# One shared wait for the score matmuls of a pair of MoBA heads

## The chip, the cores and the metric

The kernel runs on one core of a Trainium2 chip. The metric is the device time of one execution in microseconds (us), as the median of several runs. Engines are named as in the profile: PE is TensorE (PEld its weight loads), DVE is VectorE, ACT is ScalarE, POOL is GpSimd, SP is SyncE, whose queue issues the DMAs.

## The reference, cut to what matters

The reference is a two-layer decoder trunk on 256 tokens of width 1024. A layer normalises its input, modulates it by a conditioning vector, projects it by one wide matrix, runs two groups of attention heads, gates their outputs, projects back, normalises again and adds the result to its input.

The change concerns one of the two groups, the eight MoBA heads of width 64. The sequence is 256 and the MoBA block is 256, so every query has its own block alone, and for these heads the reference comes down to causal softmax attention with a linear position bias:

```python
s_own = jnp.einsum('hqd,hkd->hqk', q, k_own)
d_own = t[:, None] - pos[None, :]
s_own = jnp.where(d_own >= 0, s_own - slope_m[:, None, None] * d_own, NEG)
p = softmax(s_own)
o_m = jnp.einsum('hqb,hbd->hqd', p, v_own)
```

The other group, eight NSA heads, computes three such attentions a head (compressed, selected, window) and mixes them by gates.

## The kernel before, in words

All values are fp32. The large projections (helper `mm3`, L400 to L402) take three matmuls a product, from a high and a low part of each operand; weights come by DMA into `raw` (7 buffers) and are split by ACT (`hi`, L365) and DVE (`lo`, L373, or both parts on DVE, L367 and L373). While the first layer runs, the second layer's conditioning is computed too (the weights `w_ada`, by DVE at L234 and by PE at L217, L241 and L253).

Attention goes by blocks of two heads. There are four MoBA blocks a layer (`moba_block`) and four NSA blocks (`nsa_block`). The two heads of a MoBA block lie in partitions 0 to 63 and 64 to 127 of the same tile `qm` and `km`, so head 0 uses one half of PE's rows and head 1 the other. Queries come in two tiles of 128. A block issues four score matmuls (L636) in this order: head 0 with query tile 0 (128 keys), head 1 with query tile 0, head 0 with query tile 1 (256 keys), head 1 with query tile 1. The profile counts two records for each, so a block has eight. Head 0's scores go to one PSUM bank and head 1's to another; both have the tag `sc`, of which there are two banks, so a block takes both. Then `softmax` reads each head's bank in two spans by DVE (L546, with the bias and the row minimum), ACT does the exponentials (L549), and DVE or ACT scales (L560, L557). `transposed` puts the scaled scores through PE (L569) and copies them back (L575 on ACT, L573 on DVE), four matmuls multiply them by the values (L647), and `gate_out` multiplies by the gate (L656, L659, L660).

The banks `sc` are shared with the NSA blocks (L604, L605), with the compression (`ph` in `compress_out`, `sc` in `cmp_attn`) and with the last third of an output projection. A bank is free once its last reader is done. A matmul that writes a bank waits for that reader alone; so before the change head 0's matmuls wait for the reader of their bank, and head 1's for the reader of theirs.

Apart from the start of the first layer, whose order is written out by hand, the order on each engine is made by a planner when the kernel is built: in a model of the run it lets each engine take, of the instructions that are ready by then, the one that was traced first. `PLAN` gives the order of tracing, and steps lie far apart in it, so PE fills waits with matmuls of projections traced later. On the chip every engine goes through its own list in order. The helper `beside(mms, lasts)` makes each matmul of a list depend on the finished instructions `lasts`, and keeps the matmuls in their order among themselves; it does not forbid other matmuls between them. The other callers give it real `lasts` (`self.scaled`, `self.copies`); the score matmuls of MoBA give it an empty list.

Of the kernel before, what the change touches and what calls it, by code (L numbers as in the profile page):

```python
# [26 lines left out]
T_PAD = 16  # L27
# [41 lines left out]
class Trunk:  # L69
    def __init__(self, tc, ins, out):  # L70
        self.tc = tc
        self.nc = tc.nc
        self.I = ins
        self.out = out
        self.depth = ins["w_ada"].shape[0]
        self.n = 0
        self.how = ""
        self.used = set()
        self.copies, self.scaled = [], []
        self.parts, self.pv, self.z = {}, {}, [None, None]  # L80

    def pool(self, name, bufs=1, **kw):
# [371 lines left out]
    def compress_out(self, l):  # L454
        nc = self.nc
        sp = self.sp
        R = self.cmpR
        w1v = []
        for n in ("w_ck1", "w_cv1"):
            w1 = self.tl(self.rp, [P, 16, HD], "raw")  # L460
            nc.sync.dma_start(w1, self.I[n][l].rearrange("(m p) c -> p m c", p=P))
            w1v.append(w1)
        w2 = self.tl(self.mp, [P, P], "w2")
        nc.sync.dma_start(w2[0:HD, 0:HD], self.I["w_ck2"][l])
        nc.sync.dma_start(w2[0:HD, HD:P], self.I["w_ck2"][l])
        nc.sync.dma_start(w2[HD:P, 0:HD], self.I["w_cv2"][l])
        ph = self.tl(self.ps, [P, 512], "sc", bufs=2)
        for m in range(16):
            for i in range(2):
                nc.tensor.matmul(ph[i * HD:(i + 1) * HD, :33], w1v[i][:, m, :],  # L470
                                 R[:, i, m % 8, m // 8:m // 8 + 33],
                                 start=(m == 0), stop=(m == 15))
        hid = self.tl(sp, [P, 32], "hid", bufs=1)
        pb = self.tl(sp, [P, 1], "pbias", bufs=1)
        nc.vector.tensor_copy(pb, ph[:, 32:33])
        nc.vector.tensor_scalar_add(hid, ph[:, :32], pb)
        u = self.tl(sp, [P, 32], "gu", bufs=1)
        nc.vector.tensor_mul(u, hid, hid)
        nc.vector.tensor_scalar(u, u, 0.044715, 1.0, op0=OP.mult, op1=OP.add)
        nc.vector.tensor_mul(u, u, hid)  # L480
        nc.scalar.activation(u, u, AF.Tanh, scale=0.7978845608028654)
        nc.vector.tensor_scalar(u, u, 1.0, 0.5, op0=OP.add, op1=OP.mult)
        gel = self.tl(sp, [P, NG, 16], "gelu", bufs=1)
        nc.vector.tensor_mul(gel.rearrange("p g t -> p (g t)"), u, hid)
        grep = self.tl(sp, [P, NG, 4, 16], "gelr", bufs=1)
        for g in range(NG):
            nc.vector.tensor_copy(grep[HD:P, g], gel[HD:P, g:g + 1, :].broadcast_to([HD, 4, 16]))
        pk = self.tl(self.ps, [P, 512], "tr", bufs=2)
        nc.tensor.matmul(pk[:, :32], w2[0:HD, :], gel[0:HD].rearrange("p g t -> p (g t)"),
                         start=True, stop=True)  # L490
        nc.vector.tensor_copy(self.kbd[0:HD, :, 0:16],
                              pk[0:HD, :32].rearrange("p (g t) -> p g t", g=NG))
        nc.vector.tensor_copy(self.kbd[HD:P, :, 16:32],
                              pk[HD:P, :32].rearrange("p (g t) -> p g t", g=NG))
        pv = self.tl(self.ps, [P, 512], "tr", bufs=2)
        nc.tensor.matmul(pv[:, :HD], grep[HD:P].rearrange("p g j t -> p (g j t)"),
                         w2[HD:P, 0:HD], start=True, stop=True)
        self.vx = self.tl(self.mp, [P, NH, HD], "vx")
        nc.vector.tensor_tensor(
            self.vx, pv[:, :HD].unsqueeze(1).broadcast_to([P, NH, HD]),  # L500
            self.hmask.unsqueeze(2).broadcast_to([P, NH, HD]), op=OP.mult)

    def cmp_attn(self):
        nc = self.nc
        pt = self.tl(self.ps, [P, 512], "tr", bufs=2)
        for b in range(NBLK):
            nc.tensor.matmul(pt[b * 32:b * 32 + 32, :S], self.kbd[:, b // 2, :],
                             self.qn[:, b, :], start=True, stop=True)
        st = self.tl(self.wp, [P, 512], "S")
        nc.scalar.copy(st[:, :S], pt[:, :S])  # L510
        sc = self.tl(self.ps, [P, 512], "sc", bufs=2)
        for qt in range(NT):
            nc.tensor.transpose(sc[:, qt * P:(qt + 1) * P], st[:, qt * P:(qt + 1) * P], self.ident)
        n = NT * NH
        s = self.tl(self.wp, [P, n, T_PAD], "S")
        sv = s.rearrange("p n t -> p (n t)")
        nc.vector.tensor_add(sv, sc[:, :n * T_PAD], self.cbias.rearrange("p q h t -> p (q h t)"))
        mx = self.tl(self.sp, [P, n], "cmx", bufs=1)
        nc.vector.tensor_reduce(mx, s, axis=AX.X, op=OP.max)
        nc.vector.tensor_tensor(s, s, mx.unsqueeze(2).broadcast_to([P, n, T_PAD]), op=OP.subtract)  # L520
        nc.scalar.activation(sv, sv, AF.Exp)
        sm = self.tl(self.sp, [P, n], "csm", bufs=1)
        nc.vector.tensor_reduce(sm, s, axis=AX.X, op=OP.add)
        nc.vector.reciprocal(sm, sm)
        nc.vector.tensor_mul(sm, sm, self.valid.rearrange("p q h -> p (q h)"))
        nc.vector.tensor_mul(sm.rearrange("p (q h) -> p q h", q=NT),
                             sm.rearrange("p (q h) -> p q h", q=NT),
                             self.gate.rearrange("p q (h i) -> p q h i", i=3)[:, :, :, 0])
        nc.vector.tensor_mul(s, s, sm.unsqueeze(2).broadcast_to([P, n, T_PAD]))
        pt = self.tl(self.ps, [P, 512], "tr", bufs=2)  # L530
        for qt in range(NT):
            nc.tensor.transpose(pt[:, qt * P:(qt + 1) * P],
                                sv[:, qt * P:(qt + 1) * P], self.ident)
        self.pct = self.tl(self.mp, [P, S], "pct")
        nc.scalar.copy(self.pct, pt[:, :S])


    def softmax(self, sc, h, spans, w):

        nc = self.nc  # L540
        n = len(spans)
        s = self.tl(self.wp, [P, 512], "S")
        mn = self.tl(self.sp, [P, n], "mn")
        sm = self.tl(self.sp, [P, n], "sm")
        for i, (a, b) in enumerate(spans):
            nc.vector.tensor_tensor_reduce(  # L546
                out=s[:, a:b], in0=sc[:, a:b], in1=self.bias[:, h, S - (b - a):S],
                scale=-1.0, scalar=3.0e38, op0=OP.add, op1=OP.min, accum_out=mn[:, i:i + 1])
            nc.scalar.activation(s[:, a:b], s[:, a:b], AF.Exp, bias=mn[:, i:i + 1], scale=-1.0,  # L549
                                 accum_out=sm[:, i:i + 1])  # L550
        nc.vector.reciprocal(sm, sm)
        if w is not None:
            nc.vector.tensor_mul(sm, sm, w)  # L553
        for i, (a, b) in enumerate(spans):
            if b - a > P and "v" not in self.how or "s" in self.how:
                self.scaled.append(
                    nc.scalar.activation(s[:, a:b], s[:, a:b], AF.Copy, scale=sm[:, i:i + 1]))  # L557
            else:
                self.scaled.append(
                    nc.vector.tensor_scalar_mul(s[:, a:b], s[:, a:b], sm[:, i:i + 1]))  # L560
        return s
# [66 lines left out]
    def moba_block(self, b):  # L628
        nc = self.nc
        av = self.tl(self.ps, [P, 512], "av", bufs=1)  # L630
        sc = [self.tl(self.ps, [P, 512], "sc", bufs=2) for _ in range(2)]
        mms = []
        for qt in range(2):
            for j in range(2):
# [1 line left out]
                mms.append(nc.tensor.matmul(  # L636
                    sc[j][:, qt * P:P + qt * S], self.qm[rows, b, qt * P:(qt + 1) * P],
                    self.km[rows, b, :(qt + 1) * P], start=True, stop=True))
        self.beside(mms[::1], [])
        ss = [self.softmax(sc[j], 2 * b + j, [(0, P), (P, 3 * P)], None) for j in range(2)]  # L640
        pts = self.transposed([[s[:, i * P:(i + 1) * P] for i in range(3)] for s in ss],
                              self.scaled[-4:])
        mms = []
        for kt in range(2):
            for j in range(2):
                h = 2 * b + j
# [405 lines left out]
```

## Time and profile before

| what | value |
|---|---|
| median of 3 runs | 345.75 us (343.06, 345.78, 345.75) |
| the profiled execution's own time | 344.3 us |
| its span in the trace | 342.6 us |
| granted TensorE clock, mean of the span | 0.998 |
| PE busy | 327.5 us (96%) |
| DVE busy | 264.8 us (77%) |
| ACT busy | 203.0 us (59%) |
| DMA moved | 71.12 MB |

The span goes from the first to the last instruction of the program; the time is the span and some 1.7 us around it. Busy time is the union of an engine's instruction records, so matmuls that overlap count once.

### The profile page before, as it was taken

How to read it: one execution, taken by the hardware profiler on the slowest of the kernel's cores; microseconds unless marked ns; L12 is line 12 of the kernel's file. 1: busy time of each engine (PE TensorE's matmuls, PEld its weight loads, DVE VectorE, ACT ScalarE, POOL GpSimd, SP SyncE). 2: the span in 40 equal slices, each digit the busy share in tenths (PEclk: the TensorE clock that was granted, in tenths of full speed). 3: DMA queues.
4: the chain of work that ended last, by engine and by line, in shares of the span. 5: the costliest groups of instructions: out<-in, count | busy, mean ns of one | idle time of the engine just before them, and what ended most of it. 6: DMA issues, size and time to landing. Idle time of an engine off the chain costs nothing.

```text
span 342.6 us, 7585 instructions
## 1 busy us (share of the span) xinstructions
PE 327.5 (96%) x2852; PEld 294.5 (86%) x2852; DVE 264.8 (77%) x727; ACT 203.0 (59%) x506; POOL 10.2 (3%) x23
## 2 busy tenths in 40 slices
PE   8899989989999999989998999999999999999993
PEld 7689979989988887868998899998989889877992
DVE  2647686999998997878999968699899654796232
ACT  4423315866788985749376527471599935698311
POOL 2000000300000000000020100000000000000000
PEclk9999999999999999999999999999999999999999
DMA  7999999829985657699967698749557540000111
GB/s 236 317 319 355 349 346 262 237 64 330 348 275 182 223 191 239 196 312 371 284 173 226 184 200 243 214 166 346 185 162 260 194 125 0 2 0 3 64 62 61
DMA packets 72060, 71.12 MB, mean 208 GB/s; under 512 B 11440, under 2 KB 61784, under 8 KB 72024
## 3 DMA queue, kind: packets, MB, share of 16 engines
q1 hardware_dynamic: 72024, 70.65, 66.5%
q8 instruction: 22, 0.36, 0.4%
q14 instruction: 14, 0.11, 0.1%
HBM read 69.58 MB, written 1.06 MB: 206 GB/s over the span
## 4 chain that ended last, share of the span: by engine, by line
PE 68%; DVE 15%; DMA 8%; issue 4%; ACT 2%; POOL 1%; SPq 1%; DVEq 0%; POOLq 0%; ACTq 0%
PE pj L400 14%; PE pj L401 13%; PE pj L402 13%; PE tr L569 5%; DVE lo L373 4%; PE av L622 3%; DMA yL<-in_w_ada_dram 3%; PE tr L217 2%; PE sc L636 2%; DMA km<-in_w_ada_dram 2%; PE sc L604 2%; PE sc L605 2%; PE pj L858 2%; PE av L647 2%; DMA raw<-in_w_in_dram 2%
## 5 line engine op out<-in xcount | busy, mean ns | idle before, releaser
L373 DVE TENSOR_TENSOR lo<-raw,hi 128x1024 fp32r<-128x1024 f32 (+3 forms) x82 | 90.6, 1124 | 14.1 <-ACT hi L365 13.8
L400 PE MATMUL pj<-hH,lo 128*128 128x256 f32 x320 | 92.2, 288 | 0.0
L401 PE MATMUL pj<-hL,hi 128*128 128x256 f32 x320 | 91.4, 286 | 0.0
L402 PE MATMUL pj<-hH,hi 128*128 128x256 f32 x320 | 91.3, 285 | 0.0
L365 ACT CAST hi<-raw 128x1024 fp32r<-128x1024 f32 (+4 forms) x70 | 66.2, 966 | 18.3 <-PE pj L402 15.6
L400 PEld LDWEIGHTS pj<-hH,lo 128*128 128x128 f32 x320 | 61.1, 191 | 3.1 <-issue 2.3
L401 PEld LDWEIGHTS pj<-hL,hi 128*128 128x128 f32 x320 | 61.1, 191 | 1.3 <-issue 0.7
L402 PEld LDWEIGHTS pj<-hH,hi 128*128 128x128 f32 x320 | 61.1, 191 | 1.1 <-issue 0.6
L549 ACT ACTIVATE S<-S,mn 128x128 f32<-128x128 f32 (+1 forms) x96 | 42.8, 449 | 2.9 <-DVE mn L546 2.8
L234 DVE SCALAR_TENSOR_TENSOR acc<-raw,cs,acc 128x512 f32<-128x512 f32 x49 | 36.4, 744 | 2.0 <-DMA raw<-in_w_ada_dram 1.7
L546 DVE CUSTOM_DVE_ANT_0 S<-sc,bias 128x128 f32<-128x128 f32 (+1 forms) x96 | 30.9, 350 | 4.4 <-PE tr L569 2.6
L400 PE MATMUL pj<-hi,yL 128*128 128x256 f32 x112 | 31.8, 287 | 0.0
L402 PE MATMUL pj<-hi,yH 128*128 128x256 f32 x112 | 31.8, 285 | 0.0
L401 PE MATMUL pj<-lo,yH 128*128 128x256 f32 x112 | 31.7, 284 | 0.0
L575 ACT COPY PT<-tr 128x384 f32<-128x384 f32 x44 | 19.9, 480 | 12.8 <-PE tr L569 12.5
L400 PEld LDWEIGHTS pj<-hi,yL 128*128 128x128 f32 x112 | 20.9, 188 | 1.5 <-issue 1.3
L569 PE MATMUL tr<-ident,S 128*128 128x128 f32 x144 | 21.9, 278 | 0.2
L401 PEld LDWEIGHTS pj<-lo,yH 128*128 128x128 f32 x112 | 21.0, 188 | 0.6 <-issue 0.6
L402 PEld LDWEIGHTS pj<-hi,yH 128*128 128x128 f32 x112 | 21.1, 188 | 0.4 <-issue 0.4
L557 ACT ACTIVATE S<-S,sm 128x256 f32<-128x256 f32 (+1 forms) x46 | 20.2, 482 | 1.7 <-DVE sm L553 1.4
L549 ACT ACTIVATION_READ_ACCUMULATOR S<-S,mn 128x1 f32 x96 | 18.3, 191 | 0.0
L246 ACT COPY accr<-tr 128x128 f32<-128x128 f32 x12 | 3.2, 265 | 25.4 <-PE tr L241 18.4
(242 smaller groups left out, 626.5 us busy)
## 6 DMA issues: line engine op xcount, KB each, us to landing
raw<-in_w_in_dram SPq DMA_DIRECT2D x43, 512.0 KB, 4.7
raw<-in_w_ada_dram SPq DMA_DIRECT2D x32, 512.0 KB, 4.7
raw<-in_w_out_dram SPq DMA_DIRECT2D x16, 512.0 KB, 9.1
raw<-in_w_in_dram SPq DMA_DIRECT2D x9, 256.0 KB, 5.2
qs<-in_w_ada_dram SPq DMA_DIRECT2D x4, 512.0 KB, 8.8
yH<-in_w_ada_dram SPq DMA_DIRECT2D x4, 512.0 KB, 7.9
yL<-in_w_ada_dram SPq DMA_DIRECT2D x4, 512.0 KB
raw<-in_w_in_dram SPq DMA_DIRECT2D x9, 128.0 KB, 5.6
```

What stands on the lines that cost most here:

```text
L234: nc.vector.scalar_tensor_tensor(out=out, in0=raw[:, j], scalar=self.cs[:, k:k + 1], in1=out, op0=OP.mult, op1=OP.add)
L365: self.nc.scalar.copy(hi[:, :nk * n], raw[:, :nk * n])
L373: self.nc.vector.tensor_sub(lo[:, :nk * n], raw[:, :nk * n], hi[:, :nk * n].bitcast(F32))
L400: nc.tensor.matmul(out, aL, bH, start=first, stop=False)
L401: nc.tensor.matmul(out, aH, bL, start=False, stop=False)
L402: nc.tensor.matmul(out, aH, bH, start=False, stop=last)
L546: nc.vector.tensor_tensor_reduce(out=s[:, a:b], in0=sc[:, a:b], in1=self.bias[:, h, S - (b - a):S], scale=-1.0, scalar=3.0e38, op0=OP.add, ...
L549: nc.scalar.activation(s[:, a:b], s[:, a:b], AF.Exp, bias=mn[:, i:i + 1], scale=-1.0, accum_out=sm[:, i:i + 1])
L557: nc.scalar.activation(s[:, a:b], s[:, a:b], AF.Copy, scale=sm[:, i:i + 1]))
L569: mms += [nc.tensor.transpose(pt[:, i * P:(i + 1) * P], blk, self.ident) for i, blk in enumerate(blocks)]
L575: self.copies.append(nc.scalar.copy(ps, pt[:, :3 * P]))
L622: mms.append(nc.tensor.matmul(av[j * HD:(j + 1) * HD, kt * P:S], self.vsw[:, kt, vc], pts[j][:, kt * S:S + kt * P], start=False, stop=(i = ...
```

## The change

The kernel keeps a list, `self.freed`, of the last DVE instruction that reads each bank of tag `sc` in `compress_out`, `cmp_attn` and `softmax`. `moba_block` now passes the last two of that list to `beside`. They are, in the order of tracing, the last readers of the two banks. So all four score matmuls of a block depend on both readers, where each depended on the reader of its own bank.

```diff
@@ compress_out
-        nc.vector.tensor_scalar_add(hid, ph[:, :32], pb)
+        self.freed.append(nc.vector.tensor_scalar_add(hid, ph[:, :32], pb))
@@ cmp_attn
-        nc.vector.tensor_add(sv, sc[:, :n * T_PAD], self.cbias.rearrange("p q h t -> p (q h t)"))
+        self.freed.append(nc.vector.tensor_add(
+            sv, sc[:, :n * T_PAD], self.cbias.rearrange("p q h t -> p (q h t)")))
@@ softmax
-            nc.vector.tensor_tensor_reduce(
+            last = nc.vector.tensor_tensor_reduce(
...
+        self.freed.append(last)
@@ moba_block
-        self.beside(mms[::1], [])
+        self.beside(mms, self.freed[-2:])
```

No instruction that computes is added, removed or resized.

## Rows read from the trace of the kernel before

**Rows 1.** The page, span and first part: busy us (share), instructions of each engine.

```profile
span 342.6 us, 7585 instructions
...
PE 327.5 (96%) x2852; PEld 294.5 (86%) x2852; DVE 264.8 (77%) x727; ACT 203.0 (59%) x506; POOL 10.2 (3%) x23
```

**Rows 2.** Busy time by stretch of PE, PEld, DVE, ACT, POOL; clock, DMA share, GB/s.

```profile
135.00:145.00 10.00, 10.00 (x82) 7.60 (x86) 8.84 (x37) 7.86 (x27) 0.00 (x0) 1.00 0.69 234
145.00:160.00 15.00, 13.91 (x159) 11.31 (x152) 13.22 (x39) 9.01 (x28) 0.00 (x0) 1.00 0.97 322
160.00:175.00 15.00, 14.99 (x136) 13.37 (x135) 13.78 (x29) 7.73 (x19) 0.55 (x1) 1.00 0.91 276
175.00:200.00 25.00, 23.22 (x189) 22.44 (x189) 23.68 (x47) 14.12 (x37) 2.93 (x3) 1.00 0.64 182
...
290.00:300.00 10.00, 9.94 (x76) 8.20 (x74) 8.22 (x43) 6.71 (x21) 0.00 (x0) 1.00 0.01 2
300.00:315.00 15.00, 14.74 (x129) 11.49 (x125) 13.20 (x57) 13.06 (x45) 0.00 (x0) 1.00 0.01 2
```

**Rows 3.** Timeline of PE around a split block: start, duration, line, tiles, count.

```profile
138.61 0.28 PE L401 MATMUL pj<-hL,hi 128*128 128x256 f32 x1
138.82 0.48 PE L636 MATMUL sc<-km,qm 64*128 64x128 f32 x2
139.23 0.39 PE L402 MATMUL pj<-hH,hi 128*128 128x256 f32 x1
139.46 0.28 PE L400 MATMUL pj<-hH,lo 128*128 128x256 f32 x1
139.57 0.28 PE L401 MATMUL pj<-hL,hi 128*128 128x256 f32 x1
...
139.90 0.92 PE L636 MATMUL sc<-km,qm 64*128 64x128 f32 x6
140.75 0.38 PE L400 MATMUL pj<-hH,lo 128*128 128x256 f32 x1
```

**Rows 4.** Timeline of PE, a block of the second layer in one run.

```profile
300.68 0.93 PE L636 MATMUL sc<-km,qm 64*128 64x128 f32 x8
301.53 0.87 PE L622 MATMUL av<-PT,vsw 128*64 128x256 f32 x8
```

**Rows 5.** Timeline of PE, second layer's last block: a split by a conditioning matmul.

```profile
308.83 0.49 PE L636 MATMUL sc<-km,qm 64*128 64x128 f32 x2
309.24 0.43 PE L241 MATMUL tr<-acc,ones 128*32 128x128 f32 x8
```

**Rows 6.** Timeline of PE, first layer's third block; idle before in brackets, with releaser.

```profile
151.30 0.92 PE L636 MATMUL sc<-km,qm 64*128 64x128 f32 x6
153.31 0.33 PE L253 MATMUL tr<-ident,accr 128*128 128x128 f32 x1 [1.09 <-ACT accr L246]
153.57 0.70 PE L636 MATMUL sc<-km,qm 64*128 64x256 f32 x2
154.20 0.38 PE L400 MATMUL pj<-hi,yL 128*128 128x256 f32 x1
```

**Rows 7.** Waits of PE over the span: us in total, times, longest.

```profile
PE pj L400 <- DVE hL L348: 1.0, 1, 1.0
...
PE tr L337 <- DVE wide L323: 0.7, 1, 0.7
```

**Rows 8.** Timeline of DVE: bank readers and the split that stands between two of them.

```profile
137.76 0.42 DVE L546 CUSTOM_DVE_ANT_0 S<-sc,bias 128x256 f32<-128x256 f32 x1
...
138.32 0.42 DVE L546 CUSTOM_DVE_ANT_0 S<-sc,bias 128x256 f32<-128x256 f32 x1
...
140.64 0.29 DVE L546 CUSTOM_DVE_ANT_0 S<-sc,bias 128x128 f32<-128x128 f32 x1
...
141.61 0.42 DVE L546 CUSTOM_DVE_ANT_0 S<-sc,bias 128x256 f32<-128x256 f32 x1
...
296.54 0.62 DVE L560 TENSOR_SCALAR S<-S,sm 128x256 f32<-128x256 f32 x2
298.86 0.29 DVE L546 CUSTOM_DVE_ANT_0 S<-sc,bias 128x128 f32<-128x128 f32 x1 [1.70 <-PE tr L569]
...
309.99 1.22 DVE L373 TENSOR_TENSOR lo<-raw,hi 128x1024 fp32r<-128x1024 f32 x1
```

**Rows 9.** Timeline of PE, the second layer's first split pair and the transposes after it.

```profile
293.20 0.49 PE L636 MATMUL sc<-km,qm 64*128 64x128 f32 x2
...
297.38 0.82 PE L569 MATMUL tr<-ident,S 128*128 128x128 f32 x6
```

More of the change, by code (lines that the diff above doesn't have):

```diff
@@ L78, in __init__ @@
         self.used = set()
-        self.copies, self.scaled = [], []
+        self.copies, self.scaled, self.freed = [], [], []
         self.parts, self.pv, self.z = {}, {}, [None, None]
```

## The prediction

> **What bounds the kernel now.** Read the page's first part first: PE is busy for 327.5 of 342.6 us, DVE for 264.8, ACT for 203.0 [rows 1]. So PE is the candidate, and what must be seen next is where PE's time is not useful, and where something else holds it. The busy time by stretch answers the second question [rows 2]. MoBA runs at 135 to 160 us in the first layer and at 293 to 312 us in the second. PE is busy 10.00 of 10 us at 135 to 145, 13.91 of 15 at 145 to 160, and 24.68 of the 25 us at 290 to 315. But from 145 to 200 us DVE is busy for 13.22 + 13.78 + 23.68 = 50.7 of 55 us, and the DMA share is 0.97 and then 0.91: in the first layer PE has company. The waits of PE say the same: it stands for DVE 1.0 us and 0.7 us at the end of that layer [rows 7].
>
> The first question is answered by PE's timeline around the score matmuls. In one run, all eight records of a block last 0.93 us and the next matmul starts 0.85 us after the first of them [rows 4]. A split block has two records, which are head 0 with query tile 0, then other work, then six records, which last 0.92 us and hold PE for the same 0.85 us [rows 3]. So the two records cost nothing inside a run, where head 1's stand beside them on the other half of the rows, and cost their own time when they stand alone.
>
> **The change, part by part.**
>
> *The appends to the list* put no instruction on the chip: 0.
>
> *The first two records move to the other six.* From the start of the projection matmul ahead of the lone pair to the start of the second one behind it are 139.46 - 138.61 = 0.85 us [rows 3]. Without the pair, two steps at the undisturbed 139.57 - 139.46 = 0.11 to 0.12 us take 0.24 us. The pair so costs 0.61 us: 0.41 us for itself (139.23 - 138.82) and 0.2 us for the two changes between matmuls of 64 and of 128 rows. Three blocks have this form, the second and fourth of the first layer's four in time and the first of the second layer's. Two more are split at conditioning matmuls, where the change of shape would be there anyway; I take only the pair's own 0.41 us (309.24 - 308.83) [rows 5]. PE's saving is 3 x 0.61 + 2 x 0.41 = 2.65 us, of which 0.61 + 0.61 + 0.41 = 1.63 us in the first layer and 1.02 us in the second. Two of the second layer's blocks are whole already [rows 4] and give 0.
>
> On these 0.2 us a rule of the Trainium skill can be weighed ("TensorEngine Tiling (Array Packing)", Tiling Modes, Key Properties): a change of tiling mode drains the engine. If a drain cost the full 0.28 us that a projection's record lasts, in place of its step of 0.12 us, each change would be 0.16 us, a pair of the first kind 0.73 us, and the sum 3.0 us. The row has 0.1 us a change, and I keep the row.
>
> *The third block of the first layer* is split otherwise: six records, then PE stands 1.09 us until ACT has copied a row for a conditioning transpose, then that transpose, then the last two records, which hold PE for 154.20 - 153.57 = 0.63 us alone [rows 6]. By then both banks have long been free (the block before read them last at 141.61 us [rows 8]), so the new dependence has nothing to hold here. The split is the planner's, which found the transpose ready between two score matmuls. I take 0. The bounds are 0 and 0.63 + 1.09 = 1.72 us, if shifted times in the planner's model close it and other work fills the wait.
>
> *The added wait.* Head 0's matmuls now wait for the reader of head 1's bank too. The two readers start 0.56 us apart, at 137.76 and 138.32 us [rows 8], and the six records already waited for the later one, so no wait is longer than one that PE has today, provided that the planner puts other work ahead. Behind the run on PE are projections; on DVE the first reader of the new scores. That reader came at 140.64 us, after the start of the six at 139.90 us and 1.4 us after the lone pair was done [rows 3, 8], since DVE had other work. In the second layer's first block the scores lie ready for 3 us and more: the pair ran at 293.20 us [rows 9], the reader starts at 298.86 us [rows 8]. So this costs 0 as long as DVE has that other work; without it the first span of a head starts up to 0.56 us later in each of eight blocks.
>
> *What PE gives back.* A saving on PE is worth its length only where PE comes last. In the first layer DVE is the next to be late: if all of the stretch up to 200 us hangs on DVE, the 1.63 us become longer waits of the kind in [rows 7], and 0 remains; if DVE and the transfers start earlier with PE, all of it remains. Between 0 and 1.63 I take 0.8, the middle, as PE's two waits for DVE (1.7 us) are the size of the saving. In the second layer the transposes at 297.38 us [rows 9] follow DVE's scaling, which ends at 296.54 + 0.62 = 297.16 us [rows 8], so 0.61 us less work ahead of them turns into about 0.4 us of waiting unless the planner puts more projections there, which it has. The last 0.41 us stand before a long run of projections. Between 0.6 and 1.02 I take 0.8.
>
> The sum is 0.8 + 0.8 = 1.6 us, with bounds of 0.6 and 2.65 us, or 4.4 us with the third block. The profiled execution took 344.3 us, 1.45 us under the median of 345.75 us; against it the forecast would be 342.7 us, and against the median, from which I count, 344.1 us.
>
> **The rivals.** *All of it and more* (faster by over 1%): the 2.65 us come off whole and the third block's 1.72 us with them, 4.4 us, which gives 341.4 us. For it speaks that PE is busy 96% and that its order is rebuilt with a shorter PE in the model; against it that DVE is at 92% from 145 to 200 us.
>
> *Nothing* (the change doesn't do what it says, or DVE eats it): the dependence only asks for an order and for readiness; it doesn't forbid that the planner puts a matmul between, as it did in the third block, where both banks were free. Or the first layer's part waits for DVE and the second's for ACT, which is busy for 13.06 of 15 us at 300 to 315 us [rows 2]. That gives 345.2 to 345.7 us.
>
> *Slower*: PE stands at the head of the run for the later bank. The planner's order is made from a model, and PE goes through it in order. Where DVE on the chip is later than in the model by more than the work that was put ahead, PE stands idle with everything behind it, and now with the two records as well. The place is where a long DVE operation comes between the two readers, such as the 1.22 us split at 309.99 us [rows 8]. Before, the pair at least ran in that time. If each of the five moved runs waits so, 5 x 1.22 = 6.1 us less the 2.65 us saved is 3.5 us, or 349.2 us. It decides once DVE lags by more than 2.65 / 5 = 0.53 us a run; against it speaks that the six already wait for the later reader today, and that PE ran 139.57 to 139.90 us without idle time up to them [rows 3].
>
> On that last point stands a rule of the Trainium skill ("TensorE: Matmul & The Clock Gate", What happens when you issue a matmul): only weight loads are pulled ahead, matmuls stay in program order. By it nothing would slip past a run that waits. The trace agrees: the projection at 154.20 us comes only after the transpose that waited 1.09 us [rows 6].
>
> **How the numbers follow.** Chances: forecast 0.42; nothing 0.20; all and more 0.25; slower 0.13. A difference of 1% is 3.5 us, about what a measurement of this kernel tells from no change. Forecast and nothing lie within it, so 0.62 for the same, 0.25 for faster, 0.13 for slower. The forecast's own range is 345.75 less 0.6 to 2.65, or 343.1 to 345.2 us. To hold the time 8 times in 10 I reach down past 341.4 us, to 341.0, and up to 347.3 us, about half way to the slower rival.
>
> **What would show it.** The new timeline of PE should have runs of eight in seven or eight of the eight blocks, each 0.93 us. The busy time of PE should be about 2.6 us less. If the first layer eats its part, the waits for DVE at 185 to 191 us grow from 1.7 us; if not, the first layer's end comes earlier. For the slower rival, PE would stand before L636 with DVE's L546 as releaser. For nothing, runs of two and six would still be there. I would be wrong altogether if the planner's new order moved work far from MoBA, such as when weights are split or a transfer is issued: then most of the difference lies in stretches in which no score matmul runs.

## The result, and the profile after

| kernel | median, us | executions | ratio to before | 95% interval |
|---|---|---|---|---|
| before | 344.58 | 15 | 1 | |
| changed | 341.32 | 15 | 0.992 | 0.9896 to 0.9944 |
| changed, timed again beside other kernels | 341.46 | 6 | 0.9898 | 0.9853 to 0.9943 |

The kernel is faster by 0.8%, some 2.8 us, within the bound of 1% and inside the range. The direction is as forecast; the size is not, since the interval (1.9 to 3.6 us) leaves out the 1.6 us.

What the planner made of the change can be read from the lists of instructions of the two programs. DVE, ACT and SP have the same lists in the same order. On PE only the places of four score matmuls differ, each by a few projections: two more of them stand ahead of each moved run. Of the five pairs that the prediction expected to close, four did: the second and the fourth block of the first layer in time, and the first and the last of the second layer. The first layer's first block is still cut by a transpose, and so is its third.

The execution profiled first carries a stretch of half clock (1.2 GHz, below), so the rows after are from the profile of the changed kernel when it was timed again. This is PE's timeline at the first layer's first block, and then at the blocks that answer to [rows 3], [rows 6], [rows 9] and [rows 5]; L636 is now L638, L647 is L649 and L569 is L571.

```profile
135.32 0.48 PE L638 MATMUL sc<-km,qm 64*128 64x128 f32 x2
135.74 0.33 PE L253 MATMUL tr<-ident,accr 128*128 128x128 f32 x1
135.99 0.92 PE L638 MATMUL sc<-km,qm 64*128 64x128 f32 x6
...
138.60 0.28 PE L401 MATMUL pj<-hL,hi 128*128 128x256 f32 x1
138.81 0.93 PE L638 MATMUL sc<-km,qm 64*128 64x128 f32 x8
139.67 0.38 PE L402 MATMUL pj<-hH,hi 128*128 128x256 f32 x1
...
150.34 0.92 PE L638 MATMUL sc<-km,qm 64*128 64x128 f32 x6
151.84 0.33 PE L253 MATMUL tr<-ident,accr 128*128 128x128 f32 x1 [0.59 <-ACT accr L246]
152.10 0.70 PE L638 MATMUL sc<-km,qm 64*128 64x256 f32 x2
...
154.93 0.93 PE L638 MATMUL sc<-km,qm 64*128 64x128 f32 x8
155.78 0.39 PE L402 MATMUL pj<-hi,yH 128*128 128x256 f32 x1
...
292.64 0.93 PE L638 MATMUL sc<-km,qm 64*128 64x128 f32 x8
293.50 0.39 PE L400 MATMUL pj<-hH,lo 128*128 128x256 f32 x1
...
295.05 0.87 PE L571 MATMUL tr<-ident,S 128*128 128x128 f32 x6
...
308.69 0.93 PE L638 MATMUL sc<-km,qm 64*128 64x128 f32 x8
309.54 0.39 PE L402 MATMUL pj<-hi,yH 128*128 128x256 f32 x1
```

Four blocks have runs of eight records of 0.93 us; the one at 135.32 us is cut by a transpose, and the one at 150.34 us as in [rows 6]. What this gave is best read by pairing each PE instruction with the same one in the trace of before and taking the difference of their starts:

```
just after                                        difference of starts, us
a wait for a first-layer transfer (at 48 us)      -0.74   not the change: the wait took 0.43, not 1.45
first layer, second block (138.00)                -1.23   -0.49
first layer, third block and its stop (151.84)    -1.47   (-1.02 at 147, then the stop 0.59, not 1.09)
first layer, fourth block (155.78)                -2.13   -0.66
compression of the second layer (236.06)          -1.88   (a wait for DVE longer by 0.17)
second layer, first block (291.23)                -2.39   -0.51
second layer, last block (309.54)                 -2.74   -0.36 in two steps
```

These are starts of the first matmul behind each run. Some projections further on, where the difference is steady again, the four steps are 0.59, 0.57, 0.58 and 0.35 us, together 2.1 us. At the last instruction the difference is -2.60 us, so 2.60 - 0.74 = 1.9 us of it are left. What went is 0.20 us of the second layer's first step, at the transposes at 295.05 us: they now wait for DVE's scaling, which didn't come earlier with PE. Its paired starts differ by -1.89 us from 289 to 297 us, as before the moved run, while PE stood at -2.47 us:

```profile
294.64 0.62 DVE L562 TENSOR_SCALAR S<-S,sm 128x256 f32<-128x256 f32 x2
```

The other steps (0.35 us lost at 147 us, 0.5 us won at the stop, 0.15 us lost at the compression) cancel here. They are differences between two executions: the stop before L253 was 1.09 us in the profile of before, 0.59 us here and 0.89 us in the one profiled first, and the wait before the compression was 0.7, 0.8 and 1.2 us. In the kernel with the first layer alone, below, that wait is 1.1 us and takes 0.4 us; but it is 1.1 us too with the second layer alone, where the first saves nothing, and 0.8 and 0.2 us in two executions of one kernel (all closed), so it doesn't follow what the first layer saves. The first layer's two steps, 1.2 us, are still there when PE reaches it at 236 us, in both kernels.

The waits of PE in this execution answer to [rows 7]:

```profile
PE pj L400 <- DVE hL L348: 1.0, 1, 1.0
...
PE tr L337 <- DVE wide L323: 0.7, 1, 0.7
```

They are the same 1.0 and 0.7 us. PE reached them earlier and didn't wait longer, so DVE came earlier with it: the paired starts of DVE differ by -0.72 us at 130 us and by -2.05 us from 163 to 192 us, and most issues of weights' transfers there by the same -2.05 us. Stretches as in [rows 2] show that DVE is no less busy there (windows of 15 and 25 us; busy PE, PEld, DVE, ACT, POOL):

```profile
160.00:175.00 15.00, 14.99 (x134) 13.81 (x135) 14.74 (x29) 7.75 (x18) 0.55 (x1) 1.00 0.91 276
175.00:200.00 25.00, 23.23 (x189) 22.45 (x188) 23.68 (x43) 13.04 (x33) 2.93 (x3) 1.00 0.67 178
```

In the execution profiled first, whose time was 343.26 us and not the median, the stop before L253 was 0.89 us. After it stand these stretches:

```profile
152.00:154.00 2.00, 2.00 (x9) 1.67 (x9) 2.00 (x12) 1.43 (x4) 0.00 (x0) 0.62 1.09 351
154.00:157.00 3.00, 3.00 (x20) 2.55 (x18) 2.05 (x5) 3.00 (x10) 0.00 (x0) 0.69 1.08 363
```

The granted clock of 0.62 and 0.69 is a part at 1.2 GHz and a part at 2.4 GHz; in the kernel before it was 1.00 here, behind a longer stop [rows 2, 6]. In the paired starts this takes the difference to before from -1.77 us at 151.5 us to -0.56 us at 156 us: 1.2 us that this one execution lost.

### The profile page after: what moved, and what is told of

It is laid out like the page before. It is cut to its first block, busy times and chain, and to the rows that moved or that the text cites. A ratio compares the mean times of both kernels' runs of the same rounds, so it can differ in the third digit from the quotient of the medians.

```text
span 341.5 us, 7584 instructions
## 1 busy us (share of the span) xinstructions
PE 327.2 (96%) x2852; PEld 294.6 (86%) x2852; DVE 264.7 (78%) x727; ACT 202.7 (59%) x506; POOL 10.2 (3%) x23
## 4 chain that ended last, share of the span: by engine, by line
PE 64%; DVE 15%; DMA 10%; issue 4%; ACT 3%; POOL 1%; SPq 1%; DVEq 0%; POOLq 0%; ACTq 0%
PE pj L400 14%; PE pj L402 13%; PE pj L401 13%; PE tr L571 5%; DMA raw<-in_w_in_dram 4%; DVE lo L373 4%; PE av L624 3%; DMA yL<-in_w_ada_dram 3%; PE tr L217 2%; PE sc L606 2%; DMA km<-in_w_ada_dram 2%; PE sc L607 2%; DVE acc L234 2%; PE sc L638 2%; DVE wide L744 1%
## 5 line engine op out<-in xcount | busy, mean ns | idle before, releaser
L402 PE MATMUL pj<-hi,yH 128*128 128x256 f32 x112 | 32.8, 294 | 0.0
L402 PEld LDWEIGHTS pj<-hi,yH 128*128 128x128 f32 x112 | 21.8, 194 | 1.2 <-issue 1.2
L400 PEld LDWEIGHTS pj<-hi,yL 128*128 128x128 f32 x112 | 21.7, 195 | 0.7 <-issue 0.7
L571 PE MATMUL tr<-ident,S 128*128 128x128 f32 x144 | 22.0, 279 | 0.2
L401 PEld LDWEIGHTS pj<-lo,yH 128*128 128x128 f32 x112 | 21.8, 195 | 0.4 <-issue 0.4
L571 PEld LDWEIGHTS tr<-ident,S 128*128 128x128 f32 x144 | 15.7, 140 | 2.9 <-issue 1.4
```

What stands on the lines that cost most here:

```text
L400: nc.tensor.matmul(out, aL, bH, start=first, stop=False)
L401: nc.tensor.matmul(out, aH, bL, start=False, stop=False)
L402: nc.tensor.matmul(out, aH, bH, start=False, stop=last)
L571: mms += [nc.tensor.transpose(pt[:, i * P:(i + 1) * P], blk, self.ident) for i, blk in enumerate(blocks)]
```

## The experiments

Theory A: a score pair that stands alone costs PE its own time, and what PE saves comes off the end whole. Theory B: it doesn't, because DVE, the transfers or PE's stop before the conditioning transpose swallow it. Ratios are to the kernel before, run beside them; 1 us is 0.0029.

| kernel | cuts left of six | median, us | ratio | 95% interval |
|---|---|---|---|---|
| first layer alone | 4 | 342.32 | 0.9945 | 0.9915 to 0.9975 |
| second layer alone | 4 | 343.43 | 0.9971 | 0.9938 to 1.0004 |
| the two others closed alone | 4 | 342.56 | 0.9984 | 0.9950 to 1.0018 |
| third block closed as well | 1 | 341.21 | 0.9894 | 0.9863 to 0.9925 |
| all closed | 0 | 340.68 | 0.9889 | 0.9848 to 0.9929 |
| all closed, again | 0 | 340.84 | 0.9877 | 0.9832 to 0.9922 |
| heads not alternating | 2 | 342.10 | 0.9935 | 0.9897 to 0.9972 |
| extra matmul ahead | 0 (two others) | 343.46 | 0.9991 | 0.9948 to 1.0034 |
| extra matmul in the middle | | 346.15 | 1.0048 | 1.0016 to 1.0080 |
| extra matmul after the first | | 346.42 | 1.0075 | 1.0042 to 1.0107 |

**One layer at a time.** `self.l` is the layer, set in `step`:

```diff
-        self.beside(mms, self.freed[-2:])
+        self.beside(mms, [] if self.l else self.freed[-2:])      # first layer alone
+        self.beside(mms, self.freed[-2:] if self.l else [])      # second layer alone
```

First layer alone:

> The new dependence in the first layer alone (two of the four pairs that the change closed). Theory A, a pair's own time on PE comes off the end whole: 0.5 to 0.6 us each, so 1.1 us less than before (ratio 0.997). Theory B, the first layer's part is swallowed by DVE and the transfers: 0 to 0.3 us less (0.999 to 1.000), and longer waits of PE for DVE at 182 to 192 us.

Second layer alone:

> The new dependence in the second layer alone (the other two pairs). Theory A: 0.36 and 0.49 us as the aligned traces show them, so 0.9 us less than before (0.9975). Theory B, where the whole difference of 2.7 us must come from here: 2.5 us less (0.993). If the first layer alone and the second alone add up to less than half of the whole change, neither holds and something else moved (the half clock that PE may get after its stop at the third block).

They took 0.0055 and 0.0029 off (1.9 and 1.0 us), together 0.0084; the whole change took 0.008 off. So the parts add up, as far as intervals of 0.3% either way can show it. The interval of the first layer alone leaves out the 0.999 to 1.000 of theory B, and PE's waits for DVE at 182 to 192 us are the same 1.0 and 0.7 us. The second layer's 1.0 us is near theory A's 0.9, and not the 2.5 us that would have to come from there if the first layer gave nothing; its interval holds no change too.

**Closing the two cuts that were left.** The score matmuls of two blocks are put behind the transpose that cut them (order on PE, no wait):

```diff
-        nc.tensor.transpose(pc[:, :P], ev, self.ident)
+        self.cols_mm = nc.tensor.transpose(pc[:, :P], ev, self.ident)
...
         self.beside(mms, self.freed[-2:])
+        if self.l == 0 and b in (1, 2):
+            self.behind(mms[0], self.cols_mm)     # a NoSync edge, as beside makes them
```

> The changed kernel, and two blocks of the first layer whose score matmuls were still split by a conditioning transpose are kept behind that transpose, so that all eight blocks go in one run. Theory A: the lone records go, 0.41 us at the second block of pairs traced first and 0.63 us at the third, so 1.0 us less than the changed kernel (ratio to before 0.989). Theory B, the stop before that transpose (0.89 us) is set by transfers and DVE and swallows what PE saves ahead of it: 0 to 0.6 us less than the changed kernel (0.990 to 0.992). PE's stop would be as long as before or longer, or filled by projections.

> All eight blocks in one run, once more and beside the changed kernel. Theory A: the two cuts that are left in the changed kernel cost what the others did, so 1.0 us less than it (0.3%). Theory B: the stop before the conditioning transpose swallows it: 0 to 0.3 us less.

The kernel for the third block alone has `b == 2`:

> The changed kernel with the third block of the first layer alone kept behind its transpose. Theory A: 0.63 us of the lone records, and some of the 0.9 us stop where projections now stand ahead of the transpose: 0.6 to 1.0 us less than the changed kernel. Theory B: 0 to 0.2 us less.

The changed kernel ran beside the last two:

> The changed kernel once more, beside the next two on the same chip, as their zero. Both theories: a ratio of 0.990 to 0.994 to before.

And the two cuts were closed in the kernel before, without the new dependence (`self.beside(mms, [])`):

> The kernel before with the two transposes moved ahead of the score matmuls that they split, and without the new dependence: the four pairs that the change closed are still alone, the two others are closed. Theory A: 0.41 + 0.63 = 1.0 us less than before (0.997), and up to 0.7 us more where projections now fill the stop before the second transpose (0.995). Theory B (the stop is set by transfers): 0 to 0.4 us less (0.999 to 1.000).

PE's timeline of the kernel with all closed, at the third block:

```profile
150.36 0.43 PE L241 MATMUL tr<-acc,ones 128*32 128x128 f32 x8
150.72 0.38 PE L400 MATMUL pj<-hi,yL 128*128 128x256 f32 x1
...
151.53 0.28 PE L400 MATMUL pj<-hi,yL 128*128 128x256 f32 x1
151.86 0.33 PE L253 MATMUL tr<-ident,accr 128*128 128x128 f32 x1
152.12 0.93 PE L642 MATMUL sc<-km,qm 64*128 64x128 f32 x8
152.97 0.38 PE L401 MATMUL pj<-lo,yH 128*128 128x256 f32 x1
```

Seven projections now stand where six score records stood, and no stop is noted before L253 here (0.41 us when this kernel was profiled again). All eight blocks go in one run. The time is 0.2 to 0.3% below the changed kernel's each time it was compared (0.9889 against 0.992, 0.9877 against 0.9898), as theory A has it, and it is the lowest median of all; but the intervals overlap, so neither theory A's 1.0 us nor theory B's 0 to 0.6 is excluded. The third block alone (0.9894 against 0.9898) doesn't settle it either. The traces show something of both: paired with the changed kernel's, starts come 0.60 us earlier from L253 to behind the third block's run in each of the three traces, and 0.32 us of it goes again at 157 us. There the transposes L571 now wait for ACT's scaling (it ends at 156.69 us and they start at 156.74 us with the third block alone). So a part is swallowed, as theory B has it, but by the wait for ACT's scaling and not by the stop. In the kernel before, the same two give 0.9984, 0.5 us: between the theories, and in its interval lie both.

**Heads not alternating.** The loops over `qt` and `j` change places:

> The changed kernel with the four score matmuls in the order head 0 tile 0, head 0 tile 1, head 1 tile 0, head 1 tile 1: still one run, but only the middle two can stand beside each other on the two halves of the rows. Theory A, what a lone pair costs is the missing neighbour: a run lasts 0.41 + 0.43 + 0.43 = 1.27 us in place of 0.85 us, eight times 0.42 is 3.4 us more than the changed kernel (ratio to before 1.002). Rival, what a split costs is the change of shape and not the neighbour: 0 to 0.5 us more than the changed kernel (0.992 to 0.994).

Here theory A's number failed. PE's timeline of that kernel:

```profile
138.30 0.28 PE L401 MATMUL pj<-hL,hi 128*128 128x256 f32 x1
138.51 0.93 PE L638 MATMUL sc<-km,qm 64*128 64x128 f32 x8
139.37 0.38 PE L402 MATMUL pj<-hH,hi 128*128 128x256 f32 x1
```

In the program's list on PE head 0's two matmuls stand ahead of head 1's two, and the run still lasts 0.93 us and holds PE for 0.86 us. So the neighbour wasn't taken away: within a run the two halves of the rows work side by side, whatever the order in which their matmuls are issued. The time meets what the rival expected, but the rival isn't shown by it.

**One extra matmul, in three places.** Each is the kernel with all closed, with one more matmul a block, and differs from the others only in where that matmul, of 128 rows, stands (it writes columns that nothing reads):

```diff
             for j in range(2):
+                if len(mms) == 0:     # ahead; 2: in the middle; 1: after the first
+                    mms.append(nc.tensor.matmul(sc[0][:, 3 * P:], self.ident, self.ident,
+                                                start=True, stop=True))
                 rows = slice(j * HD, (j + 1) * HD)
```

> The kernel with all eight blocks in one run, and in each block one additional matmul of 128 rows that writes unused columns of the block's bank, here ahead of the four score matmuls. It is the zero of a scale: this and the next two kernels differ only in where that matmul stands. Both theories: the extra matmul costs 0.2 to 0.3 us a block, so 2 us more than the kernel without it.

> The additional matmul of 128 rows stands between the second and the third score matmul, so a block is cut into two equal runs, in each of which both halves of the rows are in use. Theory A (a cut costs the missing neighbour, 0.41 us, and two changes of shape, 0.2 us): here only the changes, 8 x 0.2 = 1.6 us more than with the matmul ahead. Rival (any cut costs the same 0.6 us, whatever is left alone): 8 x 0.6 = 4.9 us more.

> The additional matmul of 128 rows stands between the first and the second score matmul, so head 0's first is alone in each block, as it was in five of eight before the change. Theory A: 8 x 0.61 = 4.9 us more than with the matmul ahead and 3.3 us more than with it in the middle. Rival (PE's saving is covered by DVE or transfers, so that the change's gain came from elsewhere): within 1 us of the two others.

PE's timeline at the first layer's second block, first with the extra matmul ahead:

```profile
137.60 0.28 PE L402 MATMUL pj<-hH,hi 128*128 128x256 f32 x1
137.72 0.38 PE L642 MATMUL sc<-ident 128*128 128x128 f32 x2
138.03 0.93 PE L645 MATMUL sc<-km,qm 64*128 64x128 f32 x8
138.89 0.38 PE L400 MATMUL pj<-hH,lo 128*128 128x256 f32 x1
```

In the middle:

```profile
139.80 0.28 PE L402 MATMUL pj<-hH,hi 128*128 128x256 f32 x1
140.01 0.49 PE L645 MATMUL sc<-km,qm 64*128 64x128 f32 x4
140.43 0.49 PE L642 MATMUL sc<-ident 128*128 128x128 f32 x2
140.85 0.70 PE L645 MATMUL sc<-km,qm 64*128 64x256 f32 x4
141.48 0.39 PE L400 MATMUL pj<-hH,lo 128*128 128x256 f32 x1
```

After the first:

```profile
138.28 0.28 PE L402 MATMUL pj<-hH,hi 128*128 128x256 f32 x1
138.49 0.48 PE L645 MATMUL sc<-km,qm 64*128 64x128 f32 x2
138.91 0.49 PE L642 MATMUL sc<-ident 128*128 128x128 f32 x2
139.32 0.92 PE L645 MATMUL sc<-km,qm 64*128 64x128 f32 x6
140.17 0.39 PE L400 MATMUL pj<-hH,lo 128*128 128x256 f32 x1
```

From the last projection ahead to the next one behind are 1.29, 1.68 and 1.89 us. The same matmuls so cost 0.39 us more when the run is cut in the middle, and 0.60 us more when a pair is left alone. The 0.61 us of [rows 3] is confirmed, but 0.39 us of it is the cut and 0.21 us the missing neighbour.

In time, the middle cut costs 1.0048 - 0.9991 = 0.0057 (2.0 us; expected 1.6) and the lone pair 0.0084 (2.9 us; expected 4.9). Between the two lie 0.9 us, where theory A expected 3.3. The extra matmul itself costs 0.9991 - 0.9889 = 0.0102 (3.5 us; expected 2), between kernels timed on different chips. Two of the eight blocks have a matmul cut off at the end in all three kernels, and there the lone pair holds PE only as long as the cut in the middle, so the trace has 6 x 0.60 + 2 x 0.39 = 4.4 us for it. In the paired starts 1.3 us of that (a difference of 1.08 us that falls to -0.23) are taken up at 145 to 147 us, where PE with the extra matmul ahead waits 0.65 us for ACT and 0.27 us in front of transposes, and with a lone pair doesn't. So a cost ahead of a stop can vanish in it. The intervals don't tell 2.0 from 2.9 us. Both are above the kernel with the matmul ahead, which theory B denied: the lone pair's interval lies clear of it, the middle one's overlaps it a little (1.0016 and 1.0034), and nine of the twelve times with the matmul ahead lie below the fastest of either.

## Why the prediction came out as it did

**Where the time is.** Right: PE was the bound, the score pair stood alone, and its place in a run is free.

**The price of a pair.** Right in size: 0.61 us were predicted and 0.57 to 0.59 us found at the three blocks with projections around; 0.41 us and 0.35 us at the second layer's last. Wrong in its parts: I put 0.2 us to the changes of shape and 0.41 us to the pair; a cut through the middle shows 0.39 us for the cut. The Trainium skill ("TensorEngine Tiling (Array Packing)", Key Properties) says that a change of tiling mode drains the engine. The trace agrees as far as that two more changes cost 0.39 us, more than the 0.2 us that I kept and than the 2 x 0.16 us that I estimated beside the rule; that a drain is what costs them, no run here shows.

**The number of pairs.** Wrong by one: five were counted, four closed. The first block of the first layer was cut by a transpose that the planner found ready, as was the third, and no bank had been waited for. The term is 2.1 us and not 2.65 us. I had seen this cause at the third block and took it there for 0, rightly, but didn't look for it at the first.

**What PE gives back.** Half of this step failed. In the first layer I let half of the saving go to DVE, 0.8 of 1.63 us. In the paired starts none of the 1.2 us went there. A busy share of 92% is no proof of a bound: what DVE works on there comes from PE, and DVE's work and the transfers moved up with PE's by the same 2.05 us, so the waits stayed at 1.0 and 0.7 us. In the second layer I let a fifth go, 0.2 of 1.02 us, at the transposes of the first moved block. That came out, in place and in size: 0.2 of 0.93 us went there, where DVE's scaling hadn't moved.

**The sum.** By the traces it is 1.2 + 0.7 = 1.9 us, where I had 0.8 + 0.8 = 1.6 us. One pair too many and a discount that wasn't due work against each other, so that the sum came as near as it did partly by luck. That the time lies inside the range is partly luck too: I counted from a median of three executions, 345.75 us, and 15 gave 344.58 us, and 341.32 us lies only 0.3 us above the lower end, which I had set for the rival *All of it and more*. The median is next to that rival's 341.4 us, but its 4.4 us did not come: the third block stayed cut, and the difference is 2.8 us.

**The rest of the difference.** The timing says 2.8 us, 1.9 to 3.6 by its interval, whose lower end is the 1.9 us of the traces. That more than that is real may be, but isn't shown. Over all comparisons, which ran on several chips, executions with a mean granted clock of at least 0.995 have medians of 343.69 us before (41) and 341.19 us after (17): 2.5 us. And 36 of 78 executions of the kernel before had a mean clock of 0.993 or less, and only 1 of 21 of the changed one. Two kept traces have such a mean, 0.993 (the changed kernel) and 0.982 (the second layer alone), and in both a stretch at 1.2 GHz follows PE's stop before L253; for the others only the mean is on record, and why they became rarer wasn't tried.

**The waits.** Right: no wait of PE before L638 is noted, and the slower rival did not come. The planner put two more projections ahead of each of the four moved runs.

**What the profile was to show.** Runs of eight in seven or eight blocks: there were six. PE's busy time 2.6 us less: it was 326.1 us in the trace above, 1.4 us less. It is no measure of the saving: records of neighbours overlap, so that a short wait counts as busy (the projection ahead of the transposes at 295.05 us has its record from 294.79 to 295.07 us).

## What to carry to other kernels

Matmuls that use half of the rows belong in one run: count the cuts in PE's timeline and price each by the step from the last full matmul ahead to the next one behind, less the undisturbed step. Look at what cuts each run before counting it as closed, as a buffer that is not free and an instruction that happens to be ready need different remedies. And before discounting a saving on the bound engine for a neighbour that is busy 90%, ask whether that neighbour's work starts from the bound engine's output; in the first layer it did, and the saving came through whole; in the second layer's first moved block DVE worked on what it already had, and a third of that block's saving became waiting.

## What the runs showed of the hardware

- Matmuls on the two halves of the rows went side by side, though all of one half were issued first: eight records in 0.93 us either way. With the heads not alternating, head 1's matmul of 128 columns (records from 138.52 and 138.74 us) started ahead of head 0's of 256 columns (from 138.83 us), which stands before it in the list. The Trainium skill says that matmuls start in strict order ("TensorE: Matmul & The Clock Gate", Part 3, The mechanism). The measurement differs between the two halves of the rows, and it decides here.
- After a stop of PE the clock fell, in one execution of the kernel with the second layer alone (2.02 us before L253, then half clock for some 10 us; the last three columns are the granted clock, the DMA share and GB/s):

```profile
150.00:152.00 2.00, 1.83 (x20) 1.10 (x18) 0.46 (x2) 0.00 (x0) 0.00 (x0) 1.00 0.99 346
152.00:154.00 2.00, 0.14 (x1) 0.15 (x1) 2.00 (x5) 1.06 (x3) 0.00 (x0) 0.96 1.09 376
154.00:156.00 2.00, 2.00 (x6) 1.13 (x6) 2.00 (x10) 1.57 (x4) 0.00 (x0) 0.50 1.09 349
...
162.00:164.00 2.00, 2.00 (x11) 2.00 (x10) 2.00 (x9) 0.62 (x3) 0.00 (x0) 0.50 0.27 100
164.00:166.00 2.00, 2.00 (x20) 2.00 (x18) 0.64 (x3) 0.96 (x3) 0.00 (x0) 0.98 0.56 147
```

  That execution took 349.11 us against a median of 343.43, 5.7 us more, which is over what the change gains. The stop's length alone doesn't decide it: the clock fell behind 0.89 us in the changed kernel and stayed at 1.00 behind 1.09 us in the kernel before [rows 2, 6]. In the profile of the kernel with all closed, above, no such stop is noted there.
